# Moving a layer norm beside the last stage's weight preparation, and a projection two steps later

## The chip, the cores and the metric

The kernel is one program on one core of a Trainium2 chip. TensorE multiplies matrices, VectorE, ScalarE and GpSimd (POOL in the profile) work on elements, and DMA queues carry data; the queue that carries nearly all of this kernel's loads is issued by SyncE (SP). The metric is device microseconds of one execution. The median of three runs before the change is 3132.01 us (3122.01 to 3132.42).

## The reference

One inference step of a two-layer streaming encoder, in float32. Its inputs are 1024 frames of a new stream (the prompt) and 64 frames of a running one (the sample), each frame 1024 wide. Each layer is a mixer followed by a feed-forward part, each with a residual and a layer norm:

```
x = layer_norm(alpha * x + mixer(x))
x = layer_norm(alpha * x + (silu(x @ w_in_gate) * (x @ w_in_up)) @ w_out)
```

Layer 0 mixes with two recurrences (RWKV-7 and gated linear attention). Layer 1 mixes with attention over 16 heads of 64 in a band of chunks, followed by a projection of 1024 by 1024 (w_o). The feed-forward part has 2816 hidden columns. The result is both streams' rows after layer 1, and the states and caches.

## The kernel before

The rows are handled in two halves. Half A is 384 prompt rows and the 64 sample rows (448 columns in the transposed products); half B is the other 640 prompt rows, in five row tiles of 128. Every float32 operand is split into a high and a low part, and each product is three matmuls: high by high, high by low, low by high. In the profile these are lines 123 to 125 where the weights stand in the array ("gps<-xh,wh", used for the feed-forward's input), and lines 134, 135 and 137 where the rows stand in the array (used for projections, "wh,xh", and for the feed-forward's output, "wh,hh").

`load_w` (line 93) loads 512 KB of raw weights through SP into one of two raw buffers (tag wr), lets ScalarE copy it to the high part (L100) and VectorE (L105), GpSimd (L107) or both subtract for the low part. High and low parts have four buffers each (tags wh and wl).

A feed-forward part (`ffn`, line 915) runs over 22 steps of 128 hidden columns, numbered from 0. It is a generator: each `next(f)` puts one more step into the program. A step is a gate product and an up product, 24 matmuls each, and the nonlinearity on ScalarE and VectorE. After steps 3, 7, 11, 15, 17 and 21 the down projection of the finished steps follows (`tsg`, line 799), whose products VectorE adds to the row tiles' accumulators (L825).

What matters here is layer 1, at the end of the program:

- Half B's attention (`attention`, scores on L1279 and L1280, transposes on L1295, values on L1321) runs over eight pairs of heads. From pair 2 on, two steps of half A's feed-forward follow each pair in the program. A pair's result is stored to a scratch tensor in memory, og_d (L1330).
- Half A's remaining steps follow. After step 16 (`self.JM = 16`) the program puts half B's projection: it loads og_d back (L213, eight loads, in the order 4 to 7 and then 0 to 3), splits it (L214), loads the five row tiles of the residual (L796, "acc<-x_d") and multiplies by w_o (`proj`, line 853; rows 512 to 1023 of w_o first, then rows 0 to 511). The second half's last column block is done tile by tile in the order 2, 0, 3, 1, 4. Behind each tile's matmuls stands its layer norm (`layer_norm`, line 860), which also transposes the tile (L896). `s_operands` (line 958; L989 to L1007, with splits on L112 and L113) makes the sums of row blocks that the last stage needs. Between the matmuls and the norm of tiles 2, 0, 3 and 1 one step of half A's feed-forward is put each time (steps 17 to 20); step 21 and its down projection come after tile 4.
- Half A's last layer norm stands in that last down projection, tile by tile; its output stores are kept in a list.
- The last stage is half B's feed-forward (`s_ffn`, line 1043), also 22 steps, called pairs below, since each makes a gate and an up column block. It uses seven block products of 12 matmuls where eight would be direct (lines 1058 to 1060), so it needs sums of weight blocks: `s_weights` (line 1016) loads two raw blocks through SP (L1022) and makes the sums on GpSimd (L1034, L1035, L1037, L1039), with the split on ScalarE (L1028) and VectorE (L1029). The order of the seven products asks for the sums T1 and T2 second and third; the split of T1 is the last of the four that a pair makes. Half A's kept stores are issued behind pair 1's weight loads.
- `turn`, in `run`, decides where a pair's weights lie. Raw weights have the two wr buffers for pairs 0 and 1; from pair 2 on, pairs alternate between these and half A's four accumulator tiles, so pairs 3, 5, 7 and so on lie in the accumulators. High and low parts have the four buffers and one more (in `hp`) for the first twelve tiles, and then one of the accumulators as well.

The order of instructions is not the program's order alone. The framework's planner walks the program with a cost model and issues on each engine what is ready, earlier program order first; each engine, and SP's queue, then runs in exactly the planned order. `issue_after(i)` forbids the planner to put the enclosed loads or stores ahead of `i` on its queue. A buffer's next user waits until its last reader is done. The norm's parameters (L867, "gb") have one buffer for all norms.

## Time and profile before

| | |
|---|---|
| median of three runs | 3132.01 us |
| the three runs | 3132.42, 3122.01, 3132.01 us |
| profiled execution | 3125.41 us |
| its span, first to last instruction | 3123.6 us |
| mean granted TensorE clock | 0.979 |
| TensorE busy | 3010.7 us (96%) |
| VectorE busy | 2016.3 us (65%) |
| GpSimd busy | 1350.6 us (43%) |
| ScalarE busy | 1263.9 us (40%) |

The profile comes from one execution. A window row gives its bounds and length, then each engine's busy time and number of instructions in it, in the order PE (matmul), PEld (weight load), DVE (VectorE), ACT (ScalarE), POOL (GpSimd), and last the granted clock, the DMA engines' busy share and GB/s. A matmul's recorded time is longer than the distance between two of them, since they are pipelined; times per matmul below are distances or window lengths over counts. A timeline row gives start, duration, engine, line, operation, output and inputs, and in brackets the idle time before it with what ended it. A row of the chain of waits gives start, duration and what ran. A row of instruction groups gives the total busy time and the mean in ns.

### The profile page before, as it was taken

How to read it: one execution, taken by the hardware profiler on the slowest of the kernel's cores; microseconds unless marked ns; L12 is line 12 of the kernel's file. 1: busy time of each engine (PE TensorE's matmuls, PEld its weight loads, DVE VectorE, ACT ScalarE, POOL GpSimd, SP SyncE). 2: the span in 40 equal slices, each digit the busy share in tenths (PEclk: the TensorE clock that was granted, in tenths of full speed). 3: DMA queues.
4: the chain of work that ended last, by engine and by line, in shares of the span. 5: the costliest groups of instructions: out<-in, count | busy, mean ns of one | idle time of the engine just before them, and what ended most of it. 6: DMA issues, size and time to landing. Idle time of an engine off the chain costs nothing.

```text
span 3123.6 us, 50022 instructions
## 1 busy us (share of the span) xinstructions
PE 3010.7 (96%) x17468; PEld 2674.1 (86%) x17468; DVE 2016.3 (65%) x4933; ACT 1263.9 (40%) x2753; POOL 1350.6 (43%) x1481
## 2 busy tenths in 40 slices
PE   8999999799999999999999999999999989899998
PEld 7878888688888888888999898899899868799987
DVE  5677875878898763375554456245666648766567
ACT  4454554344444333244442132355444424333332
POOL 2354533445455243343342233244455535755444
PEclk9999999889999999999999999999999989999999
DMA  6553434534533238534342233866455433322122
GB/s 204 141 161 113 109 112 119 150 103 111 141 109 108 85 110 279 174 98 124 115 121 98 75 102 112 250 184 175 126 149 142 135 112 103 105 90 93 66 82 75
DMA packets 297340, 395.10 MB, mean 126 GB/s; under 512 B 125376, under 2 KB 218424, under 8 KB 297088
## 3 DMA queue, kind: packets, MB, share of 16 engines
q1 hardware_dynamic: 295936, 389.28, 41.8%
q8 instruction: 138, 2.26, 0.3%
q10 hardware_dynamic: 1152, 2.62, 0.2%
q14 instruction: 114, 0.93, 0.1%
HBM read 319.44 MB, written 75.51 MB: 126 GB/s over the span
## 4 chain that ended last, share of the span: by engine, by line
PE 79%; DVE 8%; DMA 5%; issue 3%; POOL 3%; ACT 2%; SPq 1%; POOLq 0%; DVEq 0%; ACTq 0%
PE gps L123 11%; PE gps L124 11%; PE gps L125 11%; PE gps L134 8%; PE gps L135 7%; PE gps L137 7%; PE gps L1058 3%; PE gps L1059 2%; PE gps L1060 2%; PE op L1321 2%; PE tp L1295 2%; DVE t L548 1%; DVE x L550 1%; PE sps L1279 1%; PE sps L1280 1%
## 5 line engine op out<-in xcount | busy, mean ns | idle before, releaser
L107 POOL TENSOR_TENSOR wl<-wr,wh 128x512 fp32r<-128x512 f32 (+2 forms) x289 | 502.9, 1744 | 634.8 <-ACT wh L100 583.9
L123 PE MATMUL gps<-xh,wh 128*128 128x320 f32 (+1 forms) x2188 | 747.3, 342 | 8.7 <-ACT xh L214 6.0
L124 PE MATMUL gps<-xl,wh 128*128 128x320 f32 (+1 forms) x2188 | 745.8, 341 | 0.6 <-DVE xl L215 0.6
L125 PE MATMUL gps<-xh,wl 128*128 128x320 f32 (+1 forms) x2188 | 743.1, 340 | 1.2 <-DVE wl L105 0.7
L100 ACT CAST wh<-wr 128x1024 fp32r<-128x1024 f32 x352 | 367.1, 1048 | 467.2 <-PE gps L124 148.5
L105 DVE TENSOR_TENSOR wl<-wr,wh 128x512 fp32r<-128x512 f32 (+2 forms) x289 | 286.9, 993 | 246.6 <-ACT wh L100 244.5
L123 PEld LDWEIGHTS gps<-xh,wh 128*128 128x128 f32 x2188 | 414.7, 190 | 31.5 <-ACT xh L214 6.0
L125 PEld LDWEIGHTS gps<-xh,wl 128*128 128x128 f32 x2188 | 414.1, 189 | 20.0 <-DVE wl L105 1.5
L124 PEld LDWEIGHTS gps<-xl,wh 128*128 128x128 f32 x2188 | 414.1, 189 | 18.4 <-DVE xl L215 1.0
L1290 POOL TENSOR_SCALAR s<-s,mx 128x640 f32<-128x640 f32 (+5 forms) x144 | 203.4, 1413 | 282.2 <-DVE mx L1289 246.1
L134 PE MATMUL gps<-wh,xh 128*128 128x512 f32 x661 | 262.2, 401 | 9.9 <-ACT xh L214 7.0
L135 PE MATMUL gps<-wl,xh 128*128 128x512 f32 x661 | 262.6, 399 | 1.0 <-DVE wl L105 0.8
L137 PE MATMUL gps<-wh,xl 128*128 128x512 f32 x661 | 257.4, 397 | 4.8 <-DVE xl L215 4.8
L134 PE MATMUL gps<-wh,hh 128*128 128x512 f32 x572 | 226.2, 398 | 0.3 <-DVE acc L825 0.3
L135 PE MATMUL gps<-wl,hh 128*128 128x512 f32 x572 | 226.3, 397 | 0.0
L825 DVE TENSOR_TENSOR acc<-acc,gps 128x512 f32<-128x512 f32 x216 | 143.7, 679 | 90.5 <-PE gps L137 85.4
L137 PE MATMUL gps<-wh,hl 128*128 128x512 f32 x484 | 190.1, 398 | 2.9 <-DVE hl L938 2.8
L548 DVE TENSOR_TENSOR t<-lt,x 16x48 f32<-16x48 f32 (+9 forms) x540 | 152.8, 283 | 38.7 <-DMA lt<-l_d 28.4
L1288 ACT ACTIVATE s<-s,mx 128x640 f32<-128x640 f32 (+5 forms) x144 | 96.4, 670 | 176.6 <-DVE mx L1287 170.0
L134 PEld LDWEIGHTS gps<-wh,xh 128*128 128x128 f32 x661 | 125.9, 191 | 39.4 <-ACT xh L214 7.2
L137 PEld LDWEIGHTS gps<-wh,xl 128*128 128x128 f32 x661 | 124.6, 188 | 32.4 <-DVE xl L215 5.5
L135 PEld LDWEIGHTS gps<-wl,xh 128*128 128x128 f32 x661 | 126.0, 191 | 29.1 <-DVE wl L105 1.9
(355 smaller groups left out, 6320.4 us busy)
## 6 DMA issues: line engine op xcount, KB each, us to landing
wr<-in_w_fi SPq DMA_DIRECT2D x176, 512.0 KB
wr<-in_w_fo SPq DMA_DIRECT2D x88, 512.0 KB
wr<-in_w_in SPq DMA_DIRECT2D x44, 512.0 KB
wr<-in_w_qk SPq DMA_DIRECT2D x32, 512.0 KB
qs<-qd SPq DMA_DIRECT2D x32, 320.0 KB
wr<-in_w_om SPq DMA_DIRECT2D x16, 512.0 KB
wr<-in_w_v SPq DMA_DIRECT2D x16, 512.0 KB
vd<-vh SPq DMA_DIRECT2D x16, 512.0 KB
```

Of the source, the lines that this page charges most:

```text
L100: self.A.copy(hi, raw)
L105: self.V.tensor_tensor(lo[:, :h], raw[:, :h], hi[:, :h].bitcast(F32), op=ALU.subtract)
L107: self.G.tensor_tensor(lo[:, h:], raw[:, h:], hi[:, h:].bitcast(F32), op=ALU.subtract)
L123: self.T.matmul(ps, hi[:, kt, :], xh, start=(kt == 0), stop=False)
L124: self.T.matmul(ps, hi[:, kt, :], xl, start=False, stop=False)
L125: self.T.matmul(ps, lo[:, kt, :], xh, start=False, stop=(kt == nk - 1))
L134: self.T.matmul(ps, xh, wh, start=(i == 0), stop=False)
L135: self.T.matmul(ps, xh, wl, start=False, stop=(lo is None and i == n - 1))
L137: self.T.matmul(ps, cols(lo(kt)), wh, start=False, stop=(i == n - 1))
L548: V.tensor_tensor(tv, lt[:, j, w:16].unsqueeze(2).to_broadcast([m, r, w]), x[:, 0, j, 0:w].unsqueeze(1).to_broadcast([m, r, w]), op=ALU.mult)
L825: self.V.tensor_tensor(a, a, ps[:m], op=ALU.add)
L1290: G.tensor_scalar(s[:m, :nk], s[:m, :nk], mx[:m, 3:4], None, op0=ALU.mult)
```

## The change

Half B's projection moves from behind step 16 to behind step 18 of half A's feed-forward (`JM`). Step 17, the down projection of steps 16 and 17, and step 18 are thus ahead of it. Three steps are left to go between its tiles: step 19 after tile 2's matmuls, step 20 after tile 0's, step 21 with the last down projection after tile 3's. Tiles 1 and 4 have none.

The projection by w_o takes rows 0 to 511 first, and og_d is loaded in the order 0 to 7. Half A's own projection by w_o, earlier in the program, shares that line and changes order too.

Half A's last layer norm no longer stands in its down projection. The down projection only notes which tiles are finished; the norm's parameters are loaded behind pair 0's weights of the last stage, and one tile of the norm with its store is put behind the weights of each of pairs 1 to 4.

Since half A's accumulators now live until then, the weights of the last stage may use them later: raw weights from pair 7 on instead of pair 3 (`n > 11`), high and low parts from pair 6 on instead of pair 3 (`n > 23`).

```diff
--- before.py
+++ after.py
@@ -854,11 +854,10 @@
 
         xt = self.xt[hf]
         packed = self.pack(pool) if pool else None
-        for i, g in enumerate((1, 0)):
+        for i, g in enumerate((0, 1) if wname == "w_o" else (1, 0)):
             self.tsg(hf, acc, lambda nh, pr: self.a[wname][nh, pr], (2 * g, 2 * g + 1), xt.h, xt.l, i == 0, after if i else None, packed, between)
 
-    def layer_norm(self, hf, acc, which, layer, out=None, transpose=True, sums=None, later=None):
-
+    def layer_norm(self, hf, acc, which, layer, out=None, transpose=True, sums=None):
 
 
         gb = self.ap.tile([128, 2, D], F32, tag="gb", name="gb", bufs=1)
@@ -902,9 +901,7 @@
                         halves.append(p3)
             if sums is not None:
                 sums(i, *halves)
-            if out is not None and later is not None:
-                later.append(lambda: self.nc.sync.dma_start(out(t0, m), a))
-            elif out is not None:
+            if out is not None:
                 self.nc.sync.dma_start(out(t0, m), a)
 
         return tile
@@ -1046,10 +1043,8 @@
         hs, done = {}, 0
         for j in range(NHT):
             B = self.s_weights(j, layer, turn)
-            if j == 1:
-                with self.tc.issue_after(self.last_w):
-                    for store in later:
-                        store()
+            with self.tc.issue_after(self.last_w):
+                later(j)
             pa, pb, pc, pd, pe = (self.bank()[:, :320] for _ in range(5))
 
             def product(ps, xn, bn, first):
@@ -1337,7 +1332,7 @@
         self.gla_d = self.dp.tile([2, 128, 128], F32, name="gla_d", tag="gla_d")
         self.JX = 6
         self.PB, self.QB, self.turn, self.AQ = 1, 2, 0, (1, 4)
-        self.HB, self.PRE, self.JO, self.JM = 5, 4, 16, 16
+        self.HB, self.PRE, self.JO, self.JM = 5, 4, 16, 18
         es_scan, es_one, es_ps = ExitStack(), ExitStack(), ExitStack()
         self.sp_ps = es_ps.enter_context(tc.tile_pool(name="scps", bufs=1, space=PS))
         self.tpsum = lambda: self.sbank("tps")
@@ -1462,7 +1457,7 @@
             hp = es_a.enter_context(tc.tile_pool(name="hpA1", bufs=1))
             later = []
             outA = lambda t0, m: a["y_s"] if t0 == SMP else a["y_p"][t0 : t0 + m, :]
-            f = self.ffn(0, 1, acc0, hp, lambda: self.layer_norm(0, acc0, "ln2", 1, outA, transpose=False, later=later), True)
+            f = self.ffn(0, 1, acc0, hp, lambda: later.append, True)
             for hp in range(len(self.AQ), 8):
                 self.attention(1, hp, atp, parts)
                 for _ in range(2):
@@ -1475,12 +1470,12 @@
                 accp = self.ctx.enter_context(tc.tile_pool(name="accB1", bufs=1, side="right"))
                 self.xt[1] = self.xt_tiles(xbp, 1)
                 with tc.tile_pool(name="yr2", bufs=1, side="right") as yp, tc.issue_after(self.last_w):
-                    self.load_xt(1, self.og_d, (4, 5, 6, 7, 0, 1, 2, 3), pool=yp)
+                    self.load_xt(1, self.og_d, pool=yp)
                     self.paired = True
                     acc1 = self.load_acc(1, self.x_d, accp)
                 xs, sums = self.s_operands(self.ctx.enter_context(tc.tile_pool(name="sx", bufs=1, side="right")),
                                            self.ctx.enter_context(tc.tile_pool(name="st", bufs=1, side="right")))
-                self.proj(1, acc1, "w_o", self.layer_norm(1, acc1, "ln1", 1, sums=sums), between=lambda i: next(f) if i < 4 else None)
+                self.proj(1, acc1, "w_o", self.layer_norm(1, acc1, "ln1", 1, sums=sums), between=lambda i: next(f) if i in (2, 0, 3) else None)
         es_a.close()
         hp = self.ctx.enter_context(tc.tile_pool(name="hpB1", bufs=1))
         outB = lambda t0, m: a["y_p"][PA + t0 : PA + t0 + m, :]
@@ -1492,13 +1487,22 @@
             n = turns[kind]
             turns[kind] += 1
             if kind == "wr":
-                pool, tag, bufs = ((self.wp, "wr", 2), (accA, "acc", 4))[n > 3 and n // 2 % 2]
+                pool, tag, bufs = ((self.wp, "wr", 2), (accA, "acc", 4))[n > 11 and n // 2 % 2]
             else:
-                pool, tag, bufs = (((self.wp, kind, self.WB),) * 4 + ((hp, kind, 1), (accA, "acc", 4)))[n % 6 if n > 11 else n % 5]
+                pool, tag, bufs = (((self.wp, kind, self.WB),) * 4 + ((hp, kind, 1), (accA, "acc", 4)))[n % 6 if n > 23 else n % 5]
             return pool.tile([128, 8, 128], dt, tag=tag, name=kind, bufs=bufs)
 
+        def last_norm(j):
+
+            nonlocal norm
+            if j == 0:
+                norm = self.layer_norm(0, acc0, "ln2", 1, outA, transpose=False)
+            elif later:
+                norm(later.pop(0))
+
+        norm = None
         self.s_ffn(1, acc1, xs, hp, lambda j: spaces[j % 5], turn,
-                   lambda: self.layer_norm(1, acc1, "ln2", 1, outB, transpose=False), later)
+                   lambda: self.layer_norm(1, acc1, "ln2", 1, outB, transpose=False), last_norm)
 
 
 # ---- launch ----
```

## The prediction

> **What bounds the kernel now.** I read the page's head first, then TensorE's busy time in windows cut where its kind of work changes, then the chain, the waits and single queues inside the two windows with idle time.
>
> ```profile
> span 3123.6 us, 50022 instructions
> PE 3010.7 (96%) x17468; PEld 2674.1 (86%) x17468; DVE 2016.3 (65%) x4933; ACT 1263.9 (40%) x2753; POOL 1350.6 (43%) x1481
> ```
>
> TensorE is busy 96% of the span, so a change that keeps every matmul can only win idle time. The windows (PE, PEld, DVE, ACT, POOL busy with counts, then clock, DMA share, GB/s) show where that lies near the edit:
>
> ```profile
> 2420.00:2488.00 68.00, 67.63 (x372) 60.88 (x371) 42.72 (x98) 31.94 (x61) 34.90 (x28) 1.00 0.51 147
> 2488.00:2524.60 36.60, 19.64 (x110) 16.13 (x109) 16.73 (x51) 14.75 (x36) 13.99 (x8) 0.83 0.16 57
> 2524.60:2571.50 46.90, 46.90 (x192) 37.72 (x193) 20.98 (x27) 11.32 (x13) 16.48 (x10) 0.95 0.39 138
> 2591.20:2667.40 76.20, 74.88 (x370) 65.58 (x368) 69.29 (x121) 32.57 (x65) 48.79 (x46) 1.00 0.30 97
> 2667.40:2739.30 71.90, 60.43 (x360) 57.26 (x359) 52.27 (x69) 25.63 (x36) 49.80 (x36) 0.93 0.36 121
> 2761.60:2811.00 49.40, 49.40 (x338) 49.36 (x338) 37.34 (x45) 19.66 (x28) 28.91 (x22) 1.00 0.22 68
> ```
>
> First hole: from 2488.0 the last attention pair runs without feed-forward matmuls beside it, and TensorE idles 36.60 - 19.64 = 17.0 us before the projection. At the projection's clock of 0.95 some 2 us (5% of 46.90) are lost on top: 19 in all. Second hole: pairs 0 to 3 of the last stage (336 matmuls; pairs 4 to 7 show 49.40 for four, 12.35 each) take 71.90 with 24 matmuls of the down projection, at 0.227 us (below) 5.5 us: 71.9 - 49.4 - 5.5 = 17.0 lost. With 1.3 idle in 2591.2 to 2667.4 that makes 18.3. Nothing else near the edit idles.
>
> **Part A, the projection two steps later.** Step 17, its down projection and step 18 now come ahead of the projection. The down projection, and a step like either:
>
> ```profile
> 2581.20:2591.20 10.00, 10.00 (x46) 8.29 (x45) 5.91 (x9) 2.57 (x3) 2.81 (x2) 1.00 0.27 94
> 2594.90:2604.90 10.00, 9.93 (x49) 8.83 (x47) 9.82 (x19) 3.36 (x7) 4.76 (x5) 1.00 0.29 87
> ```
>
> With two such steps that is 2 x 9.9 + 10.0 = 29.8 us of filler (48 matmuls a step; 44, of 0.227 us, in the down projection) for a hole of 17.0. But the planner issues whatever is ready, so filler may be spent early again, as steps 12 to 16 were: they too stand behind the attention in program order and are all done by 2488. The attention's score matmuls, beside filler and then without, and the hole's end:
>
> ```profile
> L1279 PE MATMUL sps<-ks,qs 128*128 128x320 f32 (+1 forms) x20 | 6.8, 346 | 0.0
> ...
> L1279 PE MATMUL sps<-ks,qs 128*128 128x320 f32 (+1 forms) x11 | 3.9, 366 | 3.4 <-DVE mx L1283 3.4
> ...
> 2504.61 0.42 PE L1279 MATMUL sps<-ks,qs 128*128 128x320 f32 x1 [1.25 <-DVE mx L1283]
> ...
> 2518.49 2.18 DMA og_d<-o
> 2520.76 2.96 DMA yraw<-og_d
> 2524.59 0.79 PE gps L134
> ```
>
> Beside filler: 20 in 68.0 us, 3.4 each; alone: 11 in 16.6. With filler the 11 last until 2488.0 + 37.4 = 2525.4. The drain from the last score to the store (13.9) and from store to projection (6.1) then put the projection at 2545.4: 20.8 us later, with 29.8 less to do behind it. Gain 9.0, with 8.0 of the hole left (19.64 of attention and 29.8 of filler would fill TensorE to 2537.4). If the attention kept its lone pace the gain is the whole 19. The row with filler is nearest, but the drain can hold filler too: I take **11**. The row order I cost at nothing: all eight og_d loads go out after the store has landed (2518.49 + 2.18), rows 512 on first though they are today. Half A's projection changes its order on the same line; it lies in this window:
>
> ```profile
> 1720.00:1790.00 70.00, 70.00 (x340) 59.84 (x340) 32.44 (x43) 12.29 (x14) 18.41 (x11) 1.00 0.27 83
> ```
>
> Half B's feed-forward covers it without a gap; bare, a late operand there would cost the 6.1 us from store to projection seen above.
>
> SP's queue: the loads of steps 17 and 18 (six) pass ahead of w_o. If the two first w_o loads fall behind the eight og_d loads and five accumulator loads (3.65 and 4.40 us of issue), the projection starts 8.1 later and A falls to 3.
>
> ```profile
> 2483.05 7.03 SPq L97 DMA_DIRECT2D wr<-in_w_o  x2
> 2520.76 3.65 SPq L213 DMA_DIRECT2D yraw<-og_d  x8
> 2524.45 4.40 SPq L796 DMA_DIRECT2D acc<-x_d  x5
> ```
>
> A rule bears on the 2 us: the Trainium skill, TensorE: Matmul & The Clock Gate, section on the clock gate, says the array falls to half rate after an idle window of about 3.4 us and needs as long a busy one to recover. The 0.83 and 0.95 rows agree; by it, an og_d wait left bare keeps its 2 us, and A would be 9.
>
> **Part B, the projection's last tiles bare.** Step 21 and its down projection stood behind the last projection matmul; now they stand before tiles 1 and 4. Their norm and the sums for the pairs' operands (L113, VectorE and POOL) lose that cover. Tile 0's own latency, then the same points for tile 4:
>
> ```profile
> 2594.71 0.40 PE L137 MATMUL gps<-wh,xl 128*128 128x512 f32 x1
> ...
> 2603.63 1.73 POOL L889 TENSOR_TENSOR acc<-acc,gb 128x512 f32<-128x512 f32 x1
> 2605.42 0.77 PE L896 MATMUL gps<-ident,acc 128*128 128x128 f32 x5 [0.59 <-POOL acc L889]
> 2609.93 0.74 POOL L113 TENSOR_TENSOR S4l<-ss,S4h 128x256 fp32r<-128x256 f32 x1 [0.56 <-ACT S4h L112]
> ...
> 2634.81 0.39 PE L137 MATMUL gps<-wh,xl 128*128 128x512 f32 x1
> 2666.19 1.18 POOL L113 TENSOR_TENSOR S4l<-ss,S4h 128x256 fp32r<-128x256 f32 x1
> ```
>
> Tile 0: 2595.1 to 2610.7, 15.6 us with one chunk pair; tile 4 has two, so some 4 more: 19. Upper end: tile 4's 2635.2 to 2667.4, 32, under today's load. TensorE has two transposes and two products meanwhile, about 6: exposed 13 to 26. If the planner pulls the two tiles ahead of step 21's matmuls it is 0, since any ready matmul may go first. VectorE loses half A's norm here, so I take **13 lost**.
>
> **Part C, half A's norm beside pairs 1 to 4.** It adds and drops no arithmetic: three engines only do it later, and its four stores go out one a pair instead of together. Its cost where it stands, and the last POOL operation (L1039) of each pair's weights:
>
> ```profile
> L886 DVE SCALAR_TENSOR_TENSOR acc<-acc,mv,gb 128x512 f32<-128x512 f32 (+1 forms) x8 | 7.5, 977 | 0.0
> L891 DVE SCALAR_TENSOR_TENSOR acc<-acc,rstd,gb 128x512 f32<-128x512 f32 (+1 forms) x4 | 5.0, 1252 | 1.2 <-POOL rstd L883 1.2
> L878 DVE BATCH_NORM_STATS2 bs<-acc 128x6 f32<-128x512 f32 (+1 forms) x6 | 4.0, 677 | 0.0
> ...
> L889 POOL TENSOR_TENSOR acc<-acc,gb 128x512 f32<-128x512 f32 (+1 forms) x4 | 11.0, 2763 | 1.3 <-ACT acc L888 1.3
> L883 POOL TENSOR_TENSOR rstd<-rstd,mhalf 128x1 f32<-128x1 f32 (+1 forms) x4 | 3.5, 868 | 0.2
> L882 POOL TENSOR_SCALAR rstd<-mv 128x1 f32<-128x1 f32 (+1 forms) x4 | 3.3, 816 | 0.3
> ...
> 2669.43 1.28 POOL L1039 TENSOR_TENSOR wr<-wr 128x512 f32<-128x512 f32 x1
> 2689.82 1.27 POOL L1039 TENSOR_TENSOR wr<-wr 128x512 f32<-128x512 f32 x1
> 2710.92 1.27 POOL L1039 TENSOR_TENSOR wr<-wr 128x512 f32<-128x512 f32 x1
> 2720.85 1.31 POOL L1039 TENSOR_TENSOR wr<-wr 128x512 f32<-128x512 f32 x1
> ```
>
> A pair's weights come 20.4 and 21.1 us apart where the pairs want 12.35, with both norms on POOL and VectorE. Only pair 3's come 9.9 on: their raw tiles lay in an accumulator and were loaded early. The norm's 16.5 us of VectorE and 17.8 of POOL become about 4.1 and 4.5 a pair. VectorE, at 37.34/4 = 9.3 a pair, rises to 13.4, over 12.35 by 1.1: **5 lost** over four pairs, if only that binds. The weights' own period comes from SP's queue:
>
> ```profile
> 2695.87 0.50 SPq L906 DMA_DIRECT2D out_dram<-acc  x1
> 2696.47 0.53 SPq L1022 DMA_DIRECT2D wr<-in_w_fi  x1
> ...
> 2713.33 18.47 SPq L97 DMA_DIRECT2D wr<-in_w_fo  x4
> ```
>
> From pair 2's load to the next load into the same two buffers: 16.9. Pairs 1 to 3 at 16.9 instead of 12.35 fall 13.7 behind, but weights need no operands: B's 13 us let them run ahead. At 21.1 it is 26 - 13 = 13. Half A's norm parameters (gb, one buffer) are now loaded behind pair 0's weights and wait until half B's norm has let the buffer go; pair 1's loads may queue behind them on SP. That would take the 13 us of lead away and make it 14. So C loses 5 (0 to 14). Each store is a new wait on SP: behind it queue the next pair's loads, then ScalarE's casts; 2695.87 is such a store, late by the norm. B and C lose 18 against 18.3 today: nothing won, nothing lost.
>
> A rule speaks against C: the Trainium skill, SBUF — State Buffer, section Who interferes with whom, has a VectorE instruction with two SBUF inputs and a GpSimd read block each other for their whole length. The same addition (L889) took 1.73 us in tile 0's chain and 2.76 on average above, which agrees. By it each tile beside a pair would pay about 1 us more: 4 on C.
>
> **Part D, fewer homes for weights.** Raw weights use the accumulators from pair 7 on, not from pair 3, since the norm still needs them. New on two buffers are pairs 3, 5 and 6 (3 is in C). Pairs 5 and 6 lose 2 x (16.9 - 12.35) = 9.1. Pair 4's weights are done early today:
>
> ```profile
> 2751.54 1.30 POOL L1039 TENSOR_TENSOR wr<-wr 128x512 f32<-128x512 f32 x1
> ```
>
> That is 8.8 us before pair 4 starts (2761.6), but with pair 3's weights later in the same buffers most of it goes. I take **6 lost**; 0 if the period is 13, 21 if it is 21 and pair 4 waits 4 too. One home less for the split weights is nothing: pairs 0 to 2 have those five today.
>
> **Sum.** 11 + 18.3 - 13 - 5 - 6 = 5 us gained. The profiled execution took 3125.41 (the span and 1.8 around it): 3125.4 - 5 = 3120. The median of the runs shown, 3132.01, lies 6.6 above it and the lowest 3.4 below.
>
> **Rivals.**
> - *The weights keep up and filler reaches the hole's end.* A is 19, C 5, D 0, B 13: 19 + 18.3 - 18 = 19, 3106. For it: B lets weights run ahead, and POOL is busy 28.91 of 49.40. Against it: the filler was burnt early before.
> - *Two raw buffers decide (slower).* Place: L1022's loads for pairs 1 to 6. At a period of 20.8 (mean of the two rows): C 3 x 8.4 - 13 = 12, D 2 x 8.4 + 4 = 21, A 9: 9 + 18.3 - 13 - 12 - 21 = -19, 3144. It decides above a period of about 18, where C and D eat the rest. For it: both rows stand under the same buffers; against: both include the norm or a late store.
> - *The hole only moves.* A is 3 (w_o loads behind og_d's), the rest as in the sum: 3 us slower, 3128. The change then doesn't do what it says for the hole.
>
> **Numbers.** Forecast 0.45, first rival 0.33, second 0.12, third 0.10. This kernel tells about 0.5%, 15.7 us, from no change. The forecast's own range is 3108 to 3132; the first rival and the execution spread reach to 3101, part of the second to 3139. Faster: the first rival and a little of the forecast, 0.37; slower: the second, 0.12; same 0.51.
>
> **What would show it.** A: 2488 to 2525 busy to over 9 tenths, an og_d wait of about 7 us or less ahead of L134. B: idle between the last down projection of half A and the first L1058, ended by L113 or L889. C and D: L1039 spaced about 17 us from pair 1 to 6, with ScalarE's casts (L1028) waiting for the loads. Spacings near 12.4 from pair 4 on, or idle under 5 us at B, would prove me too low on the gain; over 20, too high.

## The result, and the profile after

The changed kernel is slower. Its median is 3145.35 us (3140.63 to 3149.88, 7 runs) against 3128.02 us for the kernel before in the same session (3122.01 to 3134.18, 7 runs): a ratio of 1.0053, with an interval of 1.0038 to 1.0067. That is 0.53%, about 16.6 us (the two medians lie 17.3 apart). The prediction was 3120 us with a range of 3101 to 3139. One execution of a kernel below (norm held, tile 4 covered, more homes) took 4601.52 us at a granted clock of 0.579; that kernel's median of 3121.99 counts it (3121.38 without), its ratio does not.

The profiled execution of the changed kernel took 3146.58 us. The first lines of its page:

```profile
span 3144.8 us, 50007 instructions
...
PE 3014.1 (96%) x17468; PEld 2677.5 (85%) x17468; DVE 2016.0 (64%) x4933; ACT 1265.0 (40%) x2753; POOL 1344.1 (43%) x1481
```

The work is the same: 17468 matmuls, and every engine is as busy as before to within 7 us. The span is 21.2 us longer, and TensorE's busy time grew by 3.4, so idle time was added. Two numbers of before serve as a base: the attention's last part began to idle at 2488.0, and the first stretch of the last stage lost 18.3 us (the "second hole"). These are the windows of the changed kernel that answer to them (the stretch and its length; then busy time of PE, PEld, DVE, ACT and POOL with counts; then the granted clock, the DMA share and GB/s):

```profile
2425.60:2493.60 68.00, 68.00 (x375) 61.46 (x375) 42.22 (x98) 31.89 (x61) 34.45 (x28) 1.00 0.50 148
2493.60:2547.00 53.40, 43.82 (x247) 39.30 (x245) 32.64 (x74) 22.86 (x45) 23.69 (x14) 0.97 0.29 99
2547.00:2596.00 49.00, 48.94 (x205) 39.69 (x206) 24.66 (x31) 11.42 (x14) 18.17 (x11) 0.97 0.41 143
2650.30:2679.10 28.80, 10.61 (x46) 8.31 (x45) 27.37 (x48) 10.98 (x23) 17.26 (x19) 0.72 0.12 37
2650.30:2749.40 99.10, 65.05 (x370) 60.42 (x369) 74.91 (x112) 35.53 (x65) 57.37 (x55) 0.79 0.29 90
```

*Where the comparison starts.* The first row holds the same work as 2420.0 to 2488.0 before (375 and 372 matmuls in 68 us, a few at the edges aside) and ends 5.6 us later. Of the edit only the row order of half A's projection lies ahead of it, and the delay is older than that: the 9000th matmul, at 1587.2 us before, already starts 5.8 us later. So these 5.6 us belong to this one execution. From there the edit itself costs 21.2 - 5.6 = 15.6 us in the trace, against 16.6 by the ratio. All comparisons below count from this point.

*The first hole shrank.* From the end of the steps beside the attention to the projection it is now 53.4 us (before: 36.6), so the projection starts 16.8 us later, with 29.8 us less to do behind it: 13 us gained. The wait at its end, in the timeline of TensorE:

```profile
2547.07 0.80 PE L134 MATMUL gps<-wh,xh 128*128 128x512 f32 x1 [7.16 <-ACT xh L214]
```

*The second hole more than doubled.* From the end of the last covered tile to the start of the next down projection TensorE runs 370 matmuls in 99.1 us. What they need: 324 products at 49.4 / 336 = 0.147 us each (47.6), 24 of the projection at 0.227 us (5.4), and some 21 transposes at 0.13 us (2.7), together 55.7. So 43.4 us are lost, where 18.3 were lost before. The waits of TensorE there (what waited, for what; us in total, times, longest):

```profile
PE gps L895 <- POOL acc L888: 17.5, 2, 9.6
PE gps L1053 <- ACT xh L112: 6.8, 1, 6.8
PE gps L1054 <- POOL xl L113: 3.3, 1, 3.3
```

Line numbers are 5 lower than before in the last stage's function and 3 lower in `s_weights`: L1053 to L1055 are the pairs' products (L1058 to L1060 before), L895 the norm's transposes, L888 GpSimd's part of the norm. The first row is the norm of the projection's two bare tiles; the other two are the operand sums of tile 4. No row is a wait for weights: the weights did run ahead, as part B had it. Before, the largest wait of the same stretch (2645 to 2740) was one for them, L1028 being their cast:

```profile
PE gps L1058 <- ACT wh L1028: 5.7, 4, 3.1
```

The changed kernel's stretch in TensorE's order:

```profile
2663.48 1.97 PE L895 MATMUL gps<-ident,acc 128*128 128x128 f32 x8 [9.64 <-POOL acc L888]
2665.10 0.78 PE L134 MATMUL gps<-wh,xh 128*128 128x512 f32 x1
...
2676.58 1.12 PE L895 MATMUL gps<-ident,acc 128*128 128x128 f32 x4 [7.84 <-POOL acc L888]
```

Tile 1's norm stands bare for 9.64 us. Only behind its transposes come tile 4's last projection matmuls (L134 at 2665.10), and so tile 4's norm begins its own bare wait of 7.84 us after the first one has ended. The two do not overlap. Then the pairs wait, and the chain of waits says for what (start, length, what):

```profile
2678.34 5.20 DMA gb<-in_ln_w
...
2690.29 0.68 POOL rstd L882
...
2691.35 3.20 POOL rstd L882
2694.55 0.70 POOL S4l L113
...
2696.10 5.72 DVE acc L890 x2
```

L882 and L890 at these times are half A's layer norm, as is L885 behind the load of its parameters, gb. L113 is among the sums that tile 4's products want. Program order puts one norm tile beside each of the pairs 1 to 4. The planner issued all four ahead of and between tile 4's sums. It fixes the order by its cost model, and in this execution the norm was not even ready first: VectorE stands idle for gb and then takes four operations of the norm, while the cast that tile 4's next split (L113) reads was done at 2681.4.

```profile
2681.04 0.37 ACT L112 CAST xh<-gps 128x256 fp32r<-128x256 f32 x1
...
2683.57 3.78 DVE L885 SCALAR_TENSOR_TENSOR acc<-acc,mv,gb 128x512 f32<-128x512 f32 x4 [1.92 <-DMA gb<-in_ln_w]
2687.26 0.41 DVE L113 TENSOR_TENSOR xl<-gps,xh 128x256 fp32r<-128x256 f32 x1
```

The late end of the change, in the waits from 2705 to 2840: weights (L1025 is their cast) are late there, most of all in pair 6, which takes 17.0 us where the pairs 4 and 5 take 12.3 each.

```profile
PE gps L1053 <- ACT wh L1025: 3.6, 3, 2.1
```

### The profile page after: what moved, and what is told of

It is laid out like the page before. It is cut to its first block, busy times and chain, and to the rows that moved or that the text cites. A ratio compares the mean times of both kernels' runs of the same rounds, so it can differ in the third digit from the quotient of the medians.

```text
span 3144.8 us, 50007 instructions
## 1 busy us (share of the span) xinstructions
PE 3014.1 (96%) x17468; PEld 2677.5 (85%) x17468; DVE 2016.0 (64%) x4933; ACT 1265.0 (40%) x2753; POOL 1344.1 (43%) x1481
## 4 chain that ended last, share of the span: by engine, by line
PE 76%; DVE 9%; DMA 6%; issue 3%; POOL 3%; ACT 2%; SPq 1%; POOLq 0%; DVEq 0%; ACTq 0%
PE gps L123 11%; PE gps L124 11%; PE gps L125 11%; PE gps L134 7%; PE gps L135 7%; PE gps L137 7%; PE gps L1053 2%; PE gps L1054 2%; PE gps L1055 2%; PE op L1316 2%; PE tp L1290 2%; DVE t L548 1%; DVE x L550 1%; PE sps L1274 1%; PE sps L1275 1%
## 5 line engine op out<-in xcount | busy, mean ns | idle before, releaser
L107 POOL TENSOR_TENSOR wl<-wr,wh 128x512 fp32r<-128x512 f32 (+2 forms) x289 | 509.5, 1767 | 634.5 <-ACT wh L100 594.8
L105 DVE TENSOR_TENSOR wl<-wr,wh 128x512 fp32r<-128x512 f32 (+2 forms) x289 | 279.8, 969 | 254.8 <-ACT wh L100 252.8
L123 PEld LDWEIGHTS gps<-xh,wh 128*128 128x128 f32 x2188 | 414.4, 189 | 31.1 <-ACT xh L214 5.9
L124 PEld LDWEIGHTS gps<-xl,wh 128*128 128x128 f32 x2188 | 413.9, 189 | 18.6 <-DVE xl L215 1.0
L134 PE MATMUL gps<-wh,xh 128*128 128x512 f32 x661 | 262.4, 402 | 10.8 <-ACT xh L214 7.2
L134 PE MATMUL gps<-wh,hh 128*128 128x512 f32 x572 | 225.1, 398 | 0.5 <-DVE acc L825 0.3
L134 PEld LDWEIGHTS gps<-wh,xh 128*128 128x128 f32 x661 | 126.2, 191 | 40.2 <-ACT xh L214 7.3
```

The costliest lines, as they stand in the source:

```text
L105: self.V.tensor_tensor(lo[:, :h], raw[:, :h], hi[:, :h].bitcast(F32), op=ALU.subtract)
L107: self.G.tensor_tensor(lo[:, h:], raw[:, h:], hi[:, h:].bitcast(F32), op=ALU.subtract)
L123: self.T.matmul(ps, hi[:, kt, :], xh, start=(kt == 0), stop=False)
L124: self.T.matmul(ps, hi[:, kt, :], xl, start=False, stop=False)
L134: self.T.matmul(ps, xh, wh, start=(i == 0), stop=False)
```

## The experiments

The theory that this trace suggests: part A works, and three prices eat it: the two bare tiles (B), half A's norm ahead of tile 4's sums (C, by its place and not by its rate beside the pairs), and the fewer homes for weights (D). Its rivals were the prediction's own reading (C is a rate beside pairs 1 to 4), that the row order matters, and that part A is worth little by itself. All ratios are to the kernel before, run in the same session; 0.1% is 3.1 us. There were four sessions (medians of the kernel before 3126.60 to 3128.86), so kernels are compared by ratios.

| kernel | median us | ratio | interval |
|---|---|---|---|
| part A alone | 3110.13 | 0.9941 | 0.9925 to 0.9956 |
| part A and row orders | 3109.96 | 0.9944 | 0.9931 to 0.9958 |
| part A and fewer homes | 3117.65 | 0.9966 | 0.9954 to 0.9978 |
| change, norm held, tile 4 covered | 3117.82 | 0.9968 | 0.9957 to 0.9980 |
| change, tile 4 covered | 3126.99 | 1.0001 | 0.9989 to 1.0012 |
| change, norm held | 3134.29 | 1.0016 | 1.0005 to 1.0027 |
| the change | 3145.35 | 1.0053 | 1.0038 to 1.0067 |
| C and D alone | 3133.08 | 1.0017 | 1.0005 to 1.0028 |
| row orders alone | 3127.90 | 1.0001 | 0.9990 to 1.0012 |
| held, covered, more homes | 3121.99 | 0.9989 | 0.9976 to 1.0002 |
| one step later, three covers | 3122.04 | 0.9979 | 0.9969 to 0.9989 |
| part A, tiles 1 and 4 covered | 3118.61 | 0.9972 | 0.9963 to 0.9982 |
| three steps later | 3126.30 | 0.9992 | 0.9982 to 1.0003 |

### Part A alone

The kernel before, with the projection at step 18 and steps 19 and 20 behind its tiles 0 and 1. Step 21 stands behind all tiles, so tile 4 is covered. Half A's norm, the homes and the row orders are those of before.

```
-        self.HB, self.PRE, self.JO, self.JM = 5, 4, 16, 16
+        self.HB, self.PRE, self.JO, self.JM = 5, 4, 16, 18
-    ... between=lambda i: next(f) if i < 4 else None)
+    ... between=lambda i: next(f) if i in (0, 1) else None)
```

> The kernel before with the projection behind step 18 alone: steps 20 and 19 stand between the tiles (behind tiles 1 and 0), step 21 and its down projection stay behind tile 4, half A's norm stays in that down projection, the weights keep their homes, the row order is as before. In the changed kernel the projection starts 16.9 us later than before, once 5.6 us of start-up difference are taken off, with 29.8 us less to do behind it: 12.9 us won there. If that gain is real and the loss lies in the bare tiles and the moved norm, this kernel takes 3128 - 13 = 3115 (3110 to 3120). Rival, that steps moved ahead of the attention's end only move the idle time elsewhere: 3126 to 3130.

It took 3110.13 us (3103.72 to 3112.93, 6 runs), ratio 0.9941: about 18 us faster than the kernel before. Its windows of the projection and of the pairs:

```profile
2543.20:2593.30 50.10, 50.03 (x205) 40.20 (x206) 24.20 (x32) 11.41 (x14) 18.34 (x12) 0.95 0.41 143
2593.30:2658.40 65.10, 64.36 (x323) 56.30 (x322) 63.77 (x112) 30.36 (x62) 48.48 (x45) 1.00 0.26 87
2658.40:2721.90 63.50, 53.07 (x312) 50.95 (x312) 50.17 (x62) 22.86 (x33) 47.50 (x34) 0.87 0.35 120
```

Two covers do here: from 2543.2 to 2658.4 only 0.8 us are idle, though tiles 2 and 3 are bare. The third row's 312 matmuls need 45.9 at 0.147 us, so it loses 17.6: a second hole of the size of before (18.3) is still there, and part A is a gain at the first hole alone. What TensorE waits for in it is in part new, tile 4's last sum beside the low part of the weights (L1029):

```profile
PE gps L1060 <- DVE wl L1029: 3.6, 3, 3.0
PE gps L1059 <- POOL S4l L113: 3.6, 1, 3.6
```

Half A's norm, behind step 21 and so behind tile 4, comes after that sum on GpSimd (count; shortest, median and longest ns; first and last start):

```profile
2660.55 1.82 POOL L113 TENSOR_TENSOR S4l<-ss,S4h 128x256 fp32r<-128x256 f32 x1
...
L889 POOL TENSOR_TENSOR acc<-acc,gb x4: 2096/2292/4410, 2664.1 to 2687.1; 128x512 f32<-128x512 f32 x3, 64x512 f32<-64x512 f32 x1
```

### The change with half A's norm held in place

Each of the four norm tiles may be issued only behind the last VectorE, GpSimd and ScalarE operation of the pair ahead (kept in `self.mark`), so that they do lie beside pairs 1 to 4.

```
-                norm(later.pop(0))
+                with ExitStack() as st:
+                    for ins in self.mark:
+                        st.enter_context(self.tc.issue_after(ins))
+                    norm(later.pop(0))
```

> The changed kernel, with each tile of half A's norm forbidden on VectorE, GpSimd and ScalarE ahead of the last operation of the pair before it (tile 0 behind pair 0, and so on). Nothing else differs. Theory, the planner put the norm ahead of the sums of tile 4, where VectorE waits for the norm's parameters: the gaps of 3.1, 6.8 and 3.3 us between the first products of pair 0 and the half clock beside them (36 matmuls at 0.27 instead of 0.147 us) go, some 15 us: 3130 (3126 to 3135). Rival, the bare tiles 1 and 4 alone make the loss: 3142 to 3148. Rival, a norm tile beside each of pairs 1 to 4 slows these by 1 to 4 us each: it gives back 5 to 15 of it, 3135 to 3145.

### The change with tile 4 covered

```
-    ... between=lambda i: next(f) if i in (2, 0, 3) else None)
+    ... between=lambda i: next(f) if i in (0, 1, 4) else None)
```

Tile 1 is covered too, and tiles 2 and 3 are bare instead.

> The changed kernel, with steps 19, 20 and 21 behind the matmuls of tiles 0, 1 and 4 instead of 2, 0 and 3, so that step 21 and the last down projection stand between tile 4's matmuls and its norm. Nothing else differs. Theory, bare tiles: the gaps of 9.6 and 7.8 us ahead of the transposes of tiles 1 and 4 go: 3145 - 17 = 3128 (3124 to 3132). Theory, the norm alone: these gaps are then taken over by the wait for the norm's parameters, 3140 to 3146.

### Both together

> Both edits of the two kernels before. If both losses are there and add, 3145 - 15 - 17 = 3113 (3108 to 3118), and it beats the kernel before by the gain of the later projection less what two raw buffers cost pairs 5 to 7 (4.4 us in the trace). If only the bare tiles count 3128, if only the norm 3130; if the pairs' own weights then bind, as the slower rival of the prediction has it, 3122 to 3130.

The three kernels and the changed one make a square: norm free or held, tile 4 bare or covered. Measured, they took 3134.29, 3126.99 and 3117.82 us, each within the range of its first theory. Holding the norm gains 1.0053 - 1.0016 = 0.37% with tile 4 bare and 1.0001 - 0.9968 = 0.33% with it covered, 10 to 12 us. Covering tile 4 gains 0.52% with the norm free and 0.48% with it held, 15 to 16 us. Each difference is good to some 5 us by its intervals. Either price is nearly the same whether the other is paid or not. The same stretch as above (the last covered tile to the next down projection) of the kernel with the norm held:

```profile
2639.70:2727.80 88.10, 63.39 (x369) 60.14 (x368) 67.17 (x106) 33.33 (x63) 55.09 (x51) 0.86 0.25 85
```

of the one with tile 4 covered:

```profile
2650.90:2728.80 77.90, 52.52 (x333) 50.76 (x332) 53.73 (x73) 27.67 (x46) 45.48 (x37) 0.85 0.33 101
...
PE gps L1053 <- ACT xh L112: 21.7, 1, 21.7
```

and of the one with both:

```profile
2651.30:2716.70 65.40, 54.93 (x333) 52.84 (x332) 49.44 (x67) 25.28 (x43) 39.20 (x33) 0.90 0.28 91
...
PE gps L1053 <- ACT xh L112: 7.3, 1, 7.3
```

With 55.7 us needed in the first and 48.7 (324 products, 8 transposes) in the others, 32.4, 29.2 and 16.7 us are lost, and 43.4 in the changed kernel. The norm is worth 11.0 of it (tile 4 bare) and 12.5 (covered), the bare tile 14.2 (norm free) and 15.7 (held), as in the medians. With neither price paid 16.7 stay. The wait for xh tells the story of the norm: the same wait of the first pair for tile 4's operands is 21.7 us where the norm is free and 7.3 where it is held. Where GpSimd's part of the norm lies, with tile 4 covered and the norm free (operation, count; shortest, median and longest ns; first and last start):

```profile
L888 POOL TENSOR_TENSOR acc<-acc,gb x4: 1268/1501/4228, 2651.6 to 2676.7; 128x512 f32<-128x512 f32 x3, 64x512 f32<-64x512 f32 x1
```

and with the norm held:

```profile
L888 POOL TENSOR_TENSOR acc<-acc,gb x4: 1292/1518/1743, 2696.3 to 2739.8; 128x512 f32<-128x512 f32 x3, 64x512 f32<-64x512 f32 x1
```

Free, the first starts ahead of the wait (2656.4 to 2678.1) and the other three in it; held, they lie some 14 us apart beside the pairs. The load of gb is not what the price is made of: with tile 4 covered it is issued at 2638.9, well ahead, and the norm costs as much.

Beside the pairs the held norm has a price as well. From the first matmul of pair 3 to the first of pair 7 (336 products and a down projection), in the kernel before, with tile 4 covered and the norm free, and with it held:

```profile
2722.00:2798.60 76.60, 76.60 (x458) 71.81 (x457) 51.91 (x64) 28.85 (x38) 38.39 (x30) 1.00 0.25 83
...
2715.89:2799.55 83.66, 79.31 (x456) 73.48 (x457) 51.94 (x66) 28.99 (x39) 41.67 (x32) 0.98 0.24 79
...
2703.45:2791.37 87.92, 81.53 (x457) 74.92 (x457) 66.36 (x82) 30.18 (x41) 51.07 (x40) 0.96 0.33 110
```

The fewer homes cost 7.1 us there and the held norm 4.3 more (3.5 with tile 4 bare: 87.10 against 83.64 in the changed kernel).

### C and D alone

The changed kernel with the projection back at step 16, four covers and the old row orders.

```
-        self.HB, self.PRE, self.JO, self.JM = 5, 4, 16, 18
+        self.HB, self.PRE, self.JO, self.JM = 5, 4, 16, 16
-    ... between=lambda i: next(f) if i in (2, 0, 3) else None)
+    ... between=lambda i: next(f) if i < 4 else None)
...
```

> The changed kernel with the projection back at step 16, four covered tiles and the old row orders: of the change only half A's late norm (part C) and the fewer homes for raw weights (part D) are left, on the kernel before (3128.9). What I now hold: the price of C and D is what the earlier runs leave to them, about 11 us for norm tiles that VectorE and GpSimd take ahead of tile 4's operand sums, and about 8 us that stay when the tiles are held back, so some 15 to 19 us slower, 3144 to 3148, with the later tiles of half A's norm ahead of the first pairs' products as in the changed kernel. The prediction's own prices (C 5, D 6) make it 3140. If the norm hurts only because the last tiles are bare at the same time, it is within 3 us of before, 3126 to 3132.

It took 3133.08 us, ratio 1.0017: 5 us slower. This is neither the 15 to 19 that I then held nor quite the "within 3 us" of the other theory. The norm's place, in this kernel:

```profile
L888 POOL TENSOR_TENSOR acc<-acc,gb x4: 1442/2448/4708, 2667.7 to 2686.3; 128x512 f32<-128x512 f32 x3, 64x512 f32<-64x512 f32 x1
```

and in the kernel before:

```profile
L889 POOL TENSOR_TENSOR acc<-acc,gb x4: 1441/2448/4715, 2672.5 to 2691.1; 128x512 f32<-128x512 f32 x3, 64x512 f32<-64x512 f32 x1
```

First and last lie 18.6 us apart in both, 4.8 us earlier here as this whole execution is, with the same shortest, median and longest time to 7 ns. So moving the norm in program order moved nothing here: the planner issues it where it issued it before. What is left of this kernel is D, 5 us by the ratio; in its trace, too, pair 6 takes 17.0 us (12.3 before). The norm becomes a price where, as in the changed kernel, the last down projection stands ahead of tile 4's norm: half A's norm can then go ahead of tile 4's sums and takes the engines first. A later projection is not enough, since part A alone has it, with step 21 behind tile 4, and its norm follows the sums. The norm in its old place under the change's covers was not run, so whether moving it (part C) adds to this price, or step 21's place makes all of it, is not shown. My expectation had carried the 10 us of that case over to one in which it doesn't arise.

### Part A with fewer homes

```
-    ((self.wp, "wr", 2), (accA, "acc", 4))[n > 3 and n // 2 % 2]
+    ((self.wp, "wr", 2), (accA, "acc", 4))[n > 11 and n // 2 % 2]
-    (...)[n % 6 if n > 11 else n % 5]
+    (...)[n % 6 if n > 23 else n % 5]
```

> Part A alone (0.9941 of before when measured) with nothing added but the fewer homes for weights (part D): raw weights use the accumulators from pair 6 on, the split weights their sixth home from pair 4 on. In the traces of the changed kernel and of the one with held norm tiles and tile 4 covered, pairs 6 and 7 open gaps of 2.6 to 4.9 us that the kernel with part A alone doesn't have. If these are part D's price, this kernel is 4 to 6 us slower than part A alone, ratio 0.9955 to 0.996, with the same gaps at pairs 6 and 7 (the prediction's price is 6). If the gaps come from half A's late norm holding the accumulators, it is as fast as part A alone, 0.994.

It took 3117.65 us, ratio 0.9966 against 0.9941 (and 0.9944 with the row orders) without the edit: 0.22 to 0.25%, 7 to 8 us slower, somewhat more than expected; the intervals only just touch. Pairs 3 to 6, which part A alone runs in 76.57 us without a gap, and the longest wait in them:

```profile
2709.48:2791.16 81.68, 77.80 (x459) 71.76 (x458) 50.43 (x65) 28.49 (x38) 41.25 (x32) 1.00 0.23 78
...
PE gps L1058 <- ACT wh L1028: 2.1, 1, 2.1
```

The wait for the cast of the raw weights (L1028) is the one that the changed kernel shows at its end, and C and D alone shows it too. Of the 5.1 us that these pairs take longer, 3.2 lie in pair 6 and 1.9 in pair 3; by the two kernels' ratios D is 5 to 8 us. (A pair takes two raw tiles and four high and four low ones, so by the formulas the first of each kind in an accumulator is pair 7's, later than the expectation names.)

### Norm held, tile 4 covered, more homes

```
-    ((self.wp, "wr", 2), (accA, "acc", 4))[n > 11 and n // 2 % 2]
+    ((self.wp, "wr", 2), (accA, "acc", 4))[n > 5 and n // 2 % 2]
-    (...)[n % 6 if n > 23 else n % 5]
+    (...)[n % 6 if n > 11 else n % 5]
```

> The changed kernel with its norm tiles held back and tile 4 covered (3117.8 when measured before), and with the raw weights in the accumulators from pair 3 on (half A's norm has let go of them by then, as far as each tile is done) and the split weights in their sixth home from pair 2 on. If the fewer homes (part D) are the most of the 8 us that this kernel lies behind the one with part A alone, it gains 4 to 6 us: 3112 to 3114. If the 8 us are half A's norm beside the pairs, nothing changes: 3118; where the new homes only wait for the norm tiles, it may lose 2 us.

It took 3121.99 us, ratio 0.9989 against 0.9968 with the fewer homes: no gain, and rather a loss. Its waits in pairs 0 to 3, and SP's:

```profile
PE gps L1053 <- DVE c L1070: 4.7, 1, 4.7
PE gps L1053 <- ACT wh L1025: 4.6, 2, 4.1
...
SPq L1019 <- DMA out_dram<-acc: 5.9, 2, 3.6
```

and VectorE's timeline at the end of the first new wait, 4.7 us for L1070:

```profile
2705.72 1.43 DVE L885 SCALAR_TENSOR_TENSOR acc<-acc,mv,gb 128x512 f32<-128x512 f32 x2
2707.07 0.48 DVE L1070 TENSOR_TENSOR c<-gps,c 128x320 f32<-128x320 f32 x1
```

The waits at pairs 6 and 7 are gone, but two new ones of 4.7 and 4.1 us stand in pairs 2 and 3. The loads of the raw weights (L1019) now wait 5.9 us for the norm's stores out of the same accumulators, and the norm's L885 stands on VectorE right ahead of the pair's L1070. So C and D belong together here: with the norm beside the pairs, raw weights in the same accumulators brought nothing.

### The row orders

Alone, and on top of part A:

```
-    self.load_xt(1, self.og_d, (4, 5, 6, 7, 0, 1, 2, 3), pool=yp)
+    self.load_xt(1, self.og_d, pool=yp)
-        for i, g in enumerate((1, 0)):
+        for i, g in enumerate((0, 1) if wname == "w_o" else (1, 0)):
```

> The kernel before with only the row orders of the change (rows 0 to 511 first, in the projection and in the loads of the attention's output). The prediction costs them at nothing: 3128.9, ratio 1.000. If a late operand in half A's projection or in half B's first tiles shows, 3 to 6 us slower, 3132 to 3135.

> Part A alone (0.9941 of before when measured) with nothing added but the row orders (rows 0 to 511 first). By the run of the row orders alone (1.0001) they change nothing here: 0.994. If the order matters only when the projection starts right behind the store of the attention's output, with no step left to hide a late row, 3 to 5 us slower, 0.995 to 0.996.

Ratios of 1.0001 and 0.9944 (against 0.9941): nothing, in either place, to some 4 us by the intervals.

### Other amounts of filler and other covers

One step later, with steps 18, 19 and 20 behind tiles 0, 3 and 1; then part A with tiles 1 and 4 covered; then three steps later, with step 20 behind tile 1:

```
-    self.JM = 16       between: i < 4
+    self.JM = 17       between: i in (0, 3, 1)

-    self.JM = 18       between: i in (0, 1)
+    self.JM = 18       between: i in (1, 4)

-    self.JM = 18       between: i in (0, 1)
+    self.JM = 19       between: i == 1
```

> The kernel before with the projection one step later instead of two: step 17 and its down projection (9.9 + 10.0 us of matmuls) come ahead of it, and steps 18, 19 and 20 stand behind its tiles 0, 3 and 1. Part A alone with two steps gained 18.8 us (3110.1). If the hole is filled in proportion to the filler, two thirds of A's 12.9 stay, and the third cover adds nothing: 3119 to 3121. If what matters is that the down projection lies in the hole and three tiles are covered, it is as fast as with two steps: 3108 to 3112.

> Part A alone, with its two covered tiles exchanged: steps 19 and 20 stand behind tiles 1 and 4, and step 21 behind all of them, so tile 0 is bare, and step 21 stands between tile 4's norm and the first pair. If the latency of an early tile is hidden by the projection's other matmuls and only the last tiles need cover, the 10 us of gaps in pairs 0 and 1 shrink and it gains up to 6 us on part A alone: 0.992 to 0.994. If every bare tile pays its own latency, tile 0 costs 8 to 10 us and it is at 0.996 to 0.997.

> Part A alone with the projection one more step later: step 19 is filler too (9.9 us of matmuls), step 20 stands behind tile 1, step 21 behind tile 4, and tile 0 is bare. The wait for the attention's output (7 us with two steps) has something to fill it now. If it is filled, 5 to 7 us are gained there, against tile 0's bare latency of up to 10: between 0.992, where the projection's other matmuls hide that latency, and 0.996. If the filler is spent early again, beside the attention, the wait of 7 us stays and the bare tile comes on top: 0.996 to 0.997.

They took 3122.04 (0.9979), 3118.61 (0.9972) and 3126.30 us (0.9992): all three worse than part A as first built. The waits of the projection in the first:

```profile
PE gps L134 <- ACT xh L214: 6.9, 1, 6.9
PE gps L896 <- DVE acc L891: 4.5, 1, 4.5
```

in the second, beside the same 6.9 for L134:

```profile
PE gps L896 <- POOL acc L889: 6.7, 2, 3.4
PE gps L896 <- DVE acc L891: 4.5, 1, 4.5
```

and in the third:

```profile
PE gps L896 <- POOL acc L889: 10.3, 3, 6.4
PE gps L134 <- ACT xh L214: 10.1, 1, 10.1
```

The wait for the attention's output (L134) is 7 us with one step of filler or two, and 10 with three. Filler is spent beside the attention, as fast as the planner finds it ready, and never in the drain behind it. The bare tiles show their norm latency in these three kernels (L896: 4.5, 11.2 and 10.3 us), the early tiles too: the projection's other matmuls don't hide it. The expectation that only the last tiles need cover is refuted, and so is the one that the third step would fill the wait. But a bare tile need not pay. In part A alone tiles 2 and 3 are bare and no transpose waits: there half of step 19 runs ahead of tile 2's transposes and half of step 20 ahead of tile 3's, so that one step covers two tiles. One step later, tile 2 stands bare in the same place ahead of a covered tile 0, and its transposes are issued before tile 0's last matmuls and pay 4.5. Why the planner orders the two kernels differently, no run shows.

## Why the prediction was wrong, point by point

**The sum** was 11 + 18.3 - 13 - 5 - 6 = 5 us gained. The trace gives, with what was lost at the second hole in one number, 13 + 18.3 - 43.4 - 4.7 = 17 us lost (15.6 by the span), where 4.7 is what pair 6 takes longer. The step that failed is the end of part C: "B and C lose 18 against 18.3 today". They lose 43, for two reasons. The larger one is the term 18.3 itself. It was counted as won in full, as if B and C took the old hole's place. They come on top of it: with neither paid (norm held, tile 4 covered) the stretch still loses 16.7, and in part A alone 17.6, so hardly 2 of the 18.3 came back. What fills the hole has changed, from waits for weights to waits for tile 4's sums (7.3 us in one with both edits); why its size stays, no run shows. The other reason is the price of half A's norm ahead of tile 4's sums, 11.0 to 12.5 where C had 5. B's own price was near: 16.7 + 12.5 + 14.2 = 43.4.

**Part A: right.** Predicted 11, a choice above the 9 that goes with a projection at 2545.4; measured 13 in the trace, with the projection at 2547.07 - 5.6 = 2541.5. The medians give it 18 (interval 14 to 23), since the kernel with nothing else than part A gains 0.59%. The wait for the attention's output is 7.16 us, against "about 7 or less". The stretch that was to be busy to over 9 tenths, 2488 to 2525, is busy throughout (37.00 of 37.00 us from 2493.60); the idle time is the drain behind it, which no filler reached in any of the kernels that moved the projection. The w_o loads didn't fall behind og_d's, so the rival in which the hole only moves is refuted for the hole. The rule of the Trainium skill, TensorE: Matmul & The Clock Gate, section on the clock gate, had the half rate follow a wait of over 3.4 us. The trace agrees: behind the 7.16 us the window 2547 to 2596 has a clock of 0.97, some 1.5 us, so the wait kept most of its 2 us. The A of 9 that I made of it was too low all the same.

**The row order: right** at nothing, by two runs.

**Part B: the right size, but by another course.** 13 was the low end of 13 to 26. Idle ahead of the first product is 18.2 us (28.80 - 10.61). By the medians covering tile 4 instead is worth 15 to 16. What the prediction missed is the order: it costed one exposed latency for both tiles, where the trace has two, 9.64 and 7.84, one behind the other, because tile 4's matmuls are issued behind tile 1's transposes. The planner did not pull the two tiles ahead of step 21's matmuls, so the 0 at the lower end didn't come.

**Part C: wrong.** The 5 (0 to 14) was a rate, VectorE at 13.4 us a pair against 12.35, on pairs 1 to 4 (1.1 a pair, which is 4.4). As a rate it was near: held beside the pairs, the norm costs pairs 3 to 6 3.5 to 4.3 us. By the medians this can't be told from nothing: norm held and tile 4 covered is at 0.9968, part A with fewer homes and the norm in its old place at 0.9966, with some 5 us either way. But in the changed kernel the norm doesn't lie beside the pairs, and its 11 us are a matter of place. The prediction let the planner issue filler early for TensorE ("the planner issues whatever is ready") and did not apply the same sentence to VectorE and GpSimd: once the last down projection stands ahead of tile 4's norm, the norm tiles that program order puts beside pairs 1 to 4 can go early, and tile 4's sums, late for want of cover, stand behind them. It named gb, the single buffer, only for SP's queue; the chain runs 5.20 us through gb's load before VectorE can begin this norm, with tile 4's next split behind it, and 1.92 of them VectorE stands idle. The lead of the weights, which C was to use up, was real, and of no use: the first pairs wait for operands. By the rule of the Trainium skill, SBUF — State Buffer, section Who interferes with whom, C was to cost 4 more. Beside the pairs the GpSimd addition takes 1.29 to 1.74 us (norm held), no longer than the 1.73 of tile 0's chain, so the 4 us don't show; the long one, 4.228 us with the norm free, lies inside the first pair's wait (its rows are in the last section).

**Part D: right.** 6 predicted, with 0 to 21; 5 by C and D alone, 8 by part A with fewer homes. It shows in pair 6, by the cast waiting for raw weights, with 2 us in pair 3 and nothing in pair 5. The sign that was named, the last weight sum (L1039, now L1036) 17 us apart from pair 1 to 6, did not come: 25.7, 15.9, 31.1, 15.8 and 11.6.

**The rivals.** "The weights keep up and filler reaches the hole's end" had the weights of the first pairs right; filler did not reach the hole's end, where the wait of 7.16 us stays. "Two raw buffers decide (slower)", at 3144 us, has the measured time, but not its mechanism: L1022's loads are not what pairs 1 to 6 wait for, and D is 5 to 8, not 21. The slower outcome that came, the old hole staying while an engine off the critical path takes up work ahead of what the critical path needs, was on neither list. Nor did the prediction ask what part A is worth with its covers placed well: it took the cover of tiles 1 and 4 as the price of the filler, while part A alone shows that two covered tiles, and step 21 behind tile 4, leave only 0.8 us idle.

**What stays open.** Part A gains 13 us in the first hole by the trace and 18 by the medians. Single traces scatter by some 4 us: from the 14000th matmul, ahead of the first hole, to the end the kernel before takes 673.1 us, part A alone 659.3, part A with the row orders 656.0, and the row orders alone, which the medians put at nothing, 677.3. So 13 and 18 do not contradict each other, and the size is not known better. Why a second hole of 17 us stays when its waits change is not shown. Why the planner puts tile 1's transposes ahead of tile 4's matmuls is not shown either.

## What to carry to other kernels

Idle time that a change is to remove is won only when nothing else waits in its place: the hole of 18.3 us stayed at 17 with other waits in it, so book it as won only with what will fill it. An operation that has no dependence on the stage it is moved to is issued when the planner finds it ready, not where the program puts it; when a change makes the critical chain later, ask on every engine what can now go ahead of it, and tie that work down or leave it where it was. A latency that loses its cover can be paid once per tile, one after another, so the cover goes to the tiles whose successors have nothing else to run. Try the parts of a bundle one at a time: here one of its four parts was worth 0.59%, and the other edits together cost nearly twice that.

## What the runs showed of the hardware

One GpSimd operation varies more than threefold within a kernel. With tile 4 covered and the norm free, the addition L888 (128x512) takes from 1.27 to 4.23 us; the longest one, and VectorE's work in the same microseconds:

```profile
2663.35 4.23 POOL L888 TENSOR_TENSOR acc<-acc,gb 128x512 f32<-128x512 f32 x1 [0.70 <-ACT acc L887]
```

```profile
2664.11 0.41 DVE L1000 TENSOR_TENSOR sc<-st,sc 128x256 f32<-128x256 f32 x1
```

VectorE keeps 0.41 us for such a two-input operation while GpSimd's addition triples. VectorE stretches as well, elsewhere: in the changed kernel one L890 (128x512) takes 0.74 us, and the two in its chain took 5.72 together, with GpSimd's additions beside them:

```profile
2688.68 0.74 DVE L890 SCALAR_TENSOR_TENSOR acc<-acc,rstd,gb 128x512 f32<-128x512 f32 x1
```

The Trainium skill, SBUF — State Buffer, section Who interferes with whom, has such instructions of the two engines block each other; the rows agree that either may be the one to wait, but no run here separates this cause from others. Of L882, 64 rows by one column, the changed kernel's chain has 3.20 us, where the one ahead of it took 0.68 with 128 rows.

Gaps that follow each other closely cost more than their idle time. In the stretch of 99.10 us of the changed kernel 34.1 us are idle, at a granted clock of 0.79, and 43.4 are lost: a quarter more.
